# One wide selection in place of sixteen narrow ones in two expert searches, and unread products of a constant table ahead of four norms' transposes

## The chip, the cores and the metric
One core of a Trainium2 chip runs the whole kernel. The metric is the device time of one execution in microseconds. Four compute engines matter here: PE (TensorE, matrix products), DVE (VectorE), ACT (ScalarE) and POOL (GpSimd); SP issues most of the loads. PE's clock has two levels, 1.2 and 2.4 GHz, and the profile gives the granted clock as a share of the upper one (0.50 and 1.00).

## The reference, cut to what matters
256 tokens of width 1024 pass one block (stick-breaking attention, then a mixture of 32 experts) and two further layers. Each of the two layers is a mixer (attention) and a retrieval of single-neuron experts:

```python
q = (ht @ w_q).reshape(T, PEER_HEADS, 2, PEER_QDIM // 2)
s = jnp.einsum('thpd,pnd->thpn', q, sub_keys).astype(jnp.float32)
top_s, top_i = lax.top_k(s, PEER_TOPK)
cand_s = top_s[:, :, 0, :, None] + top_s[:, :, 1, None, :]
cand_i = top_i[:, :, 0, :, None] * PEER_NKEYS + top_i[:, :, 1, None, :]
best_s, best_j = lax.top_k(cand_s.reshape(T, PEER_HEADS, -1), PEER_TOPK)
experts = jnp.take_along_axis(cand_i.reshape(T, PEER_HEADS, -1), best_j, axis=-1)
gates = jax.nn.softmax(best_s, axis=-1)
```

There are 8 heads, 128 keys per half query and 16 results. Then every chosen expert's activation is `gelu(x . u[e])`, and the layer adds the gated sum of `v[e]`. Ahead of each mixer and each retrieval the tokens are normed: x divided by its root mean square, scaled and shifted.

## The kernel before, in words
Tokens lie on 128 partitions in two halves (`th`). Most products are in three passes of a 32-bit format: `mm3` (L211 to L216) takes operands split into a high and a low part. `split` (L167 to L180) makes the high part on ACT (L173) and the low part on DVE (L177) or POOL (L179).

`norm_T` (L384) makes the normed and transposed tokens. It takes the reciprocal root `r`, scales the tokens on DVE into `xs` (L395, or L405 where the sums come with the residual), transposes 16 blocks of 128 x 128 on PE by products with the identity (L412) into four PSUM banks, and from each bank ACT makes `hT` (L417) and DVE its high part `hh` (L418) and low part `hl` (L419). It runs six times: for the first mixer, for the expert mixture (bank tag "o"), for the even mixer (tag "v", with `pre`), for the odd mixer, and ahead of both retrievals ("f0" and "f1", L1437).

`peer` (L1215) is the retrieval. It has a dense form: all 16384 experts are computed in 128 tiles of 128 experts. A tile (`act_tile`, L1239) loads 128 rows of `u`, splits them (`puh` on ACT, `pul` on POOL while the route runs and on DVE later), makes 24 products of 256 columns, and stores `gelu` of the sums. `peer_route` (L1128) runs beside the first 30 tiles and finds the experts and their gates:
- eight projections of two heads' queries, each followed by the scores against the keys (L1145), copied to `s` on ACT (L1147);
- for each half of the tokens and each of 16 half-heads the 16 best scores `tv` and their places `ti` (L1155 to L1159, DVE);
- `tif`, the places as numbers (L1161);
- for each head the 256 sums `cand` (L1165), and their 16 best `bv` and places `bj` (L1172 to L1176);
- the row and column of each place, `ju` and `jf` (L1179, L1181), and for each head and each of the two a selection: compare a running number with `jf` (L1185), multiply by `tif` (L1187), sum (L1188);
- the best score subtracted (L1190), the Exp (L1192, ACT), its sum and quotient (L1194 to L1196), six transposes of `rows` (L1201), and `idx` and `gate` from them.

The order around it is set by three things. Instructions of one engine run in program order as a scheduler laid them. `tiles(N_EXP)` puts 23 tiles ahead of the Exp, which by an explicit dependency stands behind the gelu of the 23rd on ACT (L1192). `tiles(N_TR)` puts seven more ahead of the transposes of `rows`, which stand behind the last product of the seventh (`k.mm`, L1201). After the route, 64 groups of four tokens make one-hot tables `oh` (L1269) and `og`, and PE makes from them the gates of all experts; `iob` (L1226) is the table of running numbers in bf16 for that.

The lines that the steps of the prediction touch are these:

```python
        tiles(N_EXP)
        after(k, nc.scalar.activation(gt, gt, AF.Exp), k.gelu)
...
        tiles(N_TR)
...
                after(k, nc.tensor.transpose(pt[:, c * P:(c + 1) * P], rows[:, th, c, :], k.ident), k.mm)
```

Of the kernel before, what the change touches and what calls it, by code (L numbers as in the profile page):

```python
# [21 lines left out]
P = 128  # L22
# [85 lines left out]
def setup(tc, ctx, aps):  # L108
# [17 lines left out]
    for n, w in SMALL:  # L126
        setattr(k, n, sm[:, off:off + w])
        off += w
    return k
# [254 lines left out]
def norm_T(k, g, sc, sh, tag, pre=None, xs=None, hT=None):  # L384
# [7 lines left out]
    if pre is None:  # L392
        r = x_rstd(k, xs)
        for th in range(2):
            nc.vector.tensor_scalar_mul(xs[:, th, :], k.x[:, th, :], r[:, th:th + 1])  # L395
    else:
# [7 lines left out]
        for th in range(2):  # L404
            nc.vector.tensor_scalar_mul(xs[:, th, :], xg[:, th, :], r[:, 2 + th:3 + th])  # L405
        for th in range(2):
            nc.scalar.activation(k.x[:, th, :], xg[:, th, :], AF.Copy, scale=r[:, th:th + 1])
    for dp in range(4):
        ps = bank(k, tag)
        for j in range(2):  # L410
            for th in range(2):
                nc.tensor.transpose(ps[:, j * T + th * P:j * T + th * P + P],  # L412
                                    xs[:, th, (2 * dp + j) * P:(2 * dp + j + 1) * P], k.ident)
# [714 lines left out]
def peer_route(k, l, idx, gate, tiles):  # L1128
# [3 lines left out]
    with ExitStack() as st:  # L1132
# [15 lines left out]
        rows = one([P, 2, 3, P], "rows")  # L1148
        bvs = one([P, 2, 8, 16], "bv")
        for th in range(2):  # L1150
# [9 lines left out]
            tif = one([P, 8, 2, 16], f"tif{th}")  # L1160
            nc.vector.tensor_copy(tif.rearrange("p h a j -> p (h a) j"), ti)  # L1161
            tvv = tv.rearrange("p (h a) j -> p h a j", a=2)
            cand = tmp(k, pool, [P, 8, 16, 16], "cand", bufs=2)
            for h in range(8):
                nc.vector.tensor_tensor(cand[:, h], tvv[:, h, 0, :, None].to_broadcast([P, 16, 16]),  # L1165
                                        tvv[:, h, 1, None, :].to_broadcast([P, 16, 16]), ALU.add)
            bv = bvs[:, th]
            bj = one([P, 8, 16], f"bj{th}", U32)
            for h in range(8):
# [6 lines left out]
                nc.vector.max_index(bj[:, h, 8:], bv[:, h, 8:], c2)  # L1176
            for p, (op, arg) in enumerate(((ALU.logical_shift_right, 4), (ALU.bitwise_and, 15))):
                ju = one([P, 8, 16], f"ju{th}{p}", U32)
                nc.vector.tensor_scalar(ju, bj, arg, None, op0=op)  # L1179
                jf = one([P, 8, 16], f"jf{th}{p}")  # L1180
                nc.vector.tensor_copy(jf, ju)  # L1181
                o = rows[:, th, p, :].rearrange("p (h j) -> p h j", h=8)
                for h in range(8):
                    eq = tmp(k, pool, [P, 16, 16], "eq", bufs=2)
                    nc.vector.tensor_tensor(eq, k.iota[:, None, :16].to_broadcast([P, 16, 16]),  # L1185
# [318 lines left out]
```

## Time and profile before

| what | value |
|---|---|
| time, median of 3 runs | 2853.11 us (2849.63 to 2861.27) |
| time of the profiled execution | 2850.77 us |
| its span, first to last instruction | 2848.8 us |
| PE busy | 2621.2 us (92%), granted clock 0.961 on average |
| DVE busy | 1901.9 us (67%) |
| ACT busy | 1254.1 us (44%) |
| POOL busy | 391.5 us (14%) |

The span is cut by stages: the first mixer lasts to about 211 us, the expert mixture to 736, the even mixer to 905, the first retrieval to 1790, the odd mixer to 1958, and the second retrieval to the end. In each retrieval the route takes the first 190 us, the gates of all experts the next 300, the weighted sum of `v` the last 390. Busy shares are averages over these stages. What ends a wait in a stage is read from the waits and from the order in time.

### The profile page before, as it was taken

What the parts mean: (1) busy time and instruction counts of PE and PEld (TensorE: products, weight loads), DVE (VectorE), ACT (ScalarE), POOL (GpSimd) and SP (SyncE); (2) the same over time, 40 slices, a digit from 0 to 9 for tenths busy, and PEclk for the clock granted to TensorE, in tenths of its full rate; (3) what the DMA queues carried; (4) which work ended last, traced back from release to release, by engine and by line L of the source; (5) the groups of instructions that cost most, each with busy time, mean ns of one, the idle gap of its engine ahead of it and who ended that gap; (6) DMA issues with size and microseconds to landing.
All of it is one profiled execution on the core that took longest, in us unless ns stands there. A gap on an engine that the chain in (4) does not pass through costs nothing.

```text
span 2848.8 us, 47623 instructions
## 1 busy us (share of the span) xinstructions
PE 2621.2 (92%) x17205; PEld 2143.9 (75%) x17205; DVE 1901.9 (67%) x4151; ACT 1254.1 (44%) x2535; POOL 391.5 (14%) x292
## 2 busy tenths in 40 slices
PE   7998999999798968999999999798968999899998
PEld 5873343434587968999978888688958999888886
DVE  6753111111885998777787887756998777687776
ACT  3531000000555534555545555455535555555554
POOL 2220000000234551000000000224650000000000
PEclk9898999999899989999999999899989999999999
DMA  8678999997662445666797887653445666788775
GB/s 349 224 273 335 421 418 418 419 418 315 233 237 87 130 139 176 199 199 197 221 310 250 297 256 232 260 193 106 144 133 174 202 197 202 241 276 250 243 241 162
DMA packets 208150, 696.54 MB, mean 245 GB/s; under 512 B 23143, under 2 KB 91127, under 8 KB 167588
## 3 DMA queue, kind: packets, MB, share of 16 engines
q1 hardware_dynamic: 161108, 641.51, 64.8%
q10 hardware_dynamic: 46800, 51.93, 5.4%
q8 instruction: 137, 2.24, 0.3%
q14 instruction: 105, 0.86, 0.1%
HBM read 655.55 MB, written 37.78 MB: 243 GB/s over the span
## 4 chain that ended last, share of the span: by engine, by line
PE 52%; DVE 11%; DMA 3%; issue 1%; ACT 1%; ACTq 0%; SPq 0%; DVEq 0%
PE o L215 7%; PE o L216 7%; PE o L214 7%; PE u L214 7%; PE u L215 7%; PE u L216 7%; PE w L1278 3%; DVE eq L1187 2%; DMA pada<-in_ada 2%; DVE eq L1185 2%; PE w L214 2%; PE w L215 2%; PE w L216 2%; DVE adaacc L301 1%; DVE rows L1188 1%
## 5 line engine op out<-in xcount | busy, mean ns | idle before, releaser
L214 PE MATMUL u<-hh,puh 128*128 128x256 f32 x2048 | 589.7, 288 | 53.6 <-ACT puh L173 53.6
L173 ACT CAST puh<-pst 128x512 fp32r<-128x512 f32 x768 | 476.4, 621 | 292.4 <-PE u L215 271.2
L216 PE MATMUL u<-hh,pul 128*128 128x256 f32 x2048 | 578.4, 283 | 2.2 <-POOL pul L179 2.1
L215 PE MATMUL u<-hl,puh 128*128 128x256 f32 x2048 | 578.4, 282 | 0.0
L177 DVE TENSOR_TENSOR pul<-pst,puh 128x512 fp32r<-128x512 f32 x648 | 444.7, 687 | 154.0 <-ACT puh L173 153.3
L214 PEld LDWEIGHTS u<-hh,puh 128*128 128x128 f32 x2048 | 389.5, 190 | 54.0 <-ACT puh L173 54.0
L216 PEld LDWEIGHTS u<-hh,pul 128*128 128x128 f32 x2048 | 388.7, 190 | 3.5 <-POOL pul L179 2.9
L215 PEld LDWEIGHTS u<-hl,puh 128*128 128x128 f32 x2048 | 389.7, 190 | 0.0
L173 ACT CAST pvh<-pst 128x512 fp32r<-128x512 f32 x256 | 159.2, 622 | 197.6 <-ACT puh L173 117.7
L177 DVE TENSOR_TENSOR pvl<-pst,pvh 128x512 fp32r<-128x512 f32 x256 | 176.7, 690 | 67.0 <-ACT pvh L173 67.0
L214 PE MATMUL o<-pvh,pwh 128*128 128x512 f32 x512 | 202.4, 395 | 14.5 <-ACT pwh L173 14.5
L216 PE MATMUL o<-pvh,pwl 128*128 128x512 f32 x512 | 200.3, 392 | 1.5 <-DVE pwl L177 1.5
L215 PE MATMUL o<-pvl,pwh 128*128 128x512 f32 x512 | 200.4, 392 | 0.7 <-DVE pvl L177 0.7
L214 PE MATMUL o<-puh,pwh 128*128 128x512 f32 x512 | 200.0, 391 | 0.0
L215 PE MATMUL o<-pul,pwh 128*128 128x512 f32 x512 | 199.9, 390 | 0.0
L216 PE MATMUL o<-puh,pwl 128*128 128x512 f32 x512 | 199.8, 390 | 0.0
L214 PE MATMUL w<-hh,wsph 128*128 128x256 f32 x648 | 191.0, 295 | 7.7 <-ACT wsph L173 2.9
L215 PE MATMUL w<-hl,wsph 128*128 128x256 f32 x648 | 187.7, 290 | 0.0
L216 PE MATMUL w<-hh,wspl 128*128 128x256 f32 x648 | 187.2, 289 | 0.0
L179 POOL TENSOR_TENSOR pul<-pst,puh 128x512 fp32r<-128x512 f32 x120 | 172.3, 1458 | 91.2 <-ACT puh L173 89.5
L736 DVE TENSOR_TENSOR moesg<-moesg,v 128x512 f32<-128x512 f32 x16 | 11.0, 687 | 234.2 <-PE v L731 234.2
L173 ACT CAST pwh<-u 128x256 fp32r<-128x256 f32 x256 | 95.1, 371 | 125.7 <-PE o L215 101.1
(400 smaller groups left out, 5139.9 us busy)
## 6 DMA issues: line engine op xcount, KB each, us to landing
pst<-in_pu SPq DMA_DIRECT2D x256, 512.0 KB, 4.0
pst<-in_pv SPq DMA_DIRECT2D x256, 512.0 KB, 4.6
moeg<-in_moe_g SPq DMA_DIRECT2D x64, 1024.0 KB, 12.6
moeu<-in_moe_u SPq DMA_DIRECT2D x64, 1024.0 KB, 9.9
moed<-in_moe_d SPq DMA_DIRECT2D x64, 1024.0 KB, 11.6
ada<-in_ada SPq DMA_DIRECT2D x56, 1024.0 KB, 7.0
peer_a<-peerA ACTq DMA_DIRECT2D x256, 128.0 KB, 3.5
peerA<-peer_a SPq DMA_DIRECT2D x256, 128.0 KB, 3.9
```

What stands on the lines that cost most here:

```text
L173: ins = nc.scalar.copy(hi, src)
L177: nc.vector.tensor_tensor(lo, src, hi, ALU.subtract)
L179: nc.gpsimd.tensor_tensor(lo, src, hi, ALU.subtract)
L214: mm(out, lhs[0], rhs[0], start=st, stop=True, skip_group_check=True)
L215: mm(out, lhs[0], rhs[1], start=False, stop=True, skip_group_check=True)
L216: k.mm = mm(out, lhs[1], rhs[0], start=False, stop=True, skip_group_check=True)
L301: nc.vector.scalar_tensor_tensor(acc, wt[:, c, :], cond[:, kc, :1], acc, op0=ALU.mult, op1=ALU.add)
L736: nc.vector.tensor_mul(sg, sg, pgu["u"])
L1185: nc.vector.tensor_tensor(eq, k.iota[:, None, :16].to_broadcast([P, 16, 16]), jf[:, h, :, None].to_broadcast([P, 16, 16]), ALU.is_equal)
L1187: nc.vector.tensor_tensor(eq, eq, tif[:, h, p, None, :].to_broadcast([P, 16, 16]), ALU.mult)
L1188: nc.vector.tensor_reduce(o[:, h, :], eq, AX.X, ALU.add)
L1278: nc.tensor.matmul(pg[:, j], oh[:, j, 1].rearrange("p i d -> p (i d)"), og[c][:, j].rearrange("p i d -> p (i d)"), start=j == 0 and c == 0 ...
```

## The change
The diff has four parts.
- `iob`, the bf16 table of running numbers, is made once in `setup` and not once per retrieval.
- `scale_rows` takes the place of the two scalings in `norm_T`: each half of the tokens is scaled in two pieces of 512 columns, the first half on DVE and the second on ACT.
- `keep_warm` issues n products of `iob` with itself, 512 columns each, into a PSUM bank that nobody reads. They stand behind the last product before them and ahead of the transposes: 12 ahead of the expert mixture, 30 ahead of the odd mixer, 24 ahead of each retrieval.
- In `peer_route` the loops over heads go, for the sums `cand` and for the selection. The comparison and the product run over 2048 elements in bf16 (`ia` holds each running number 16 times, `tif` holds each place twice, side by side). The reduction reads `eq` with its last two dimensions exchanged. The subtraction of the best score is made for each half of the tokens, ahead of the selection.

```diff
+def scale_rows(k, dst, src, r):
+
+    for n in range(2):
+        ns = slice(n * 512, (n + 1) * 512)
+        k.nc.vector.tensor_scalar_mul(dst[:, 0, ns], src[:, 0, ns], r[:, 0:1])
+        k.nc.scalar.activation(dst[:, 1, ns], src[:, 1, ns], AF.Copy, scale=r[:, 1:2])
+
+
+def keep_warm(k, n):
+
+    ps = bank(k)
+    t = k.iob.rearrange("p i d -> p (i d)")
+    last = k.mm
+    for _ in range(n):
+        ins = k.nc.tensor.matmul(ps, t, t[:, None, :].to_broadcast([P, 4, P]), start=True, stop=True, skip_group_check=True)
+        after(k, ins, last)
+        last = ins
+    return last
...
-        for th in range(2):
-            nc.vector.tensor_scalar_mul(xs[:, th, :], k.x[:, th, :], r[:, th:th + 1])
+        scale_rows(k, xs, k.x, r)
...
+    last = keep_warm(k, warm) if warm else None
...
-            tif = one([P, 8, 2, 16], f"tif{th}")
-            nc.vector.tensor_copy(tif.rearrange("p h a j -> p (h a) j"), ti)
+            tif = one([P, 2, 8, 16, 2], f"tif{th}", BF16)
+            for p in range(2):
+                nc.vector.tensor_copy(tif[:, p], ti.rearrange("p (h a) j -> p a h j", a=2)[:, p, :, :, None].to_broadcast([P, 8, 16, 2]))
...
-            for h in range(8):
-                nc.vector.tensor_tensor(cand[:, h], tvv[:, h, 0, :, None].to_broadcast([P, 16, 16]),
-                                        tvv[:, h, 1, None, :].to_broadcast([P, 16, 16]), ALU.add)
+            nc.vector.tensor_tensor(cand, tvv[:, :, 0, :, None].to_broadcast([P, 8, 16, 16]),
+                                    tvv[:, :, 1, None, :].to_broadcast([P, 8, 16, 16]), ALU.add)
...
+            nc.vector.tensor_tensor(gt[:, th], bv, bv[:, :, 0:1].to_broadcast([P, 8, 16]), ALU.subtract)
...
-                for h in range(8):
-                    eq = tmp(k, pool, [P, 16, 16], "eq", bufs=2)
-                    nc.vector.tensor_tensor(eq, k.iota[:, None, :16].to_broadcast([P, 16, 16]),
-                                            jf[:, h, :, None].to_broadcast([P, 16, 16]), ALU.is_equal)
-                    nc.vector.tensor_tensor(eq, eq, tif[:, h, p, None, :].to_broadcast([P, 16, 16]), ALU.mult)
-                    nc.vector.tensor_reduce(o[:, h, :], eq, AX.X, ALU.add)
-        gt = rows[:, :, 2, :].rearrange("p t (h j) -> p t h j", h=8)
-        nc.vector.tensor_tensor(gt, bvs, bvs[:, :, :, 0:1].to_broadcast([P, 2, 8, 16]), ALU.subtract)
+                eq = tmp(k, pool, [P, 8, 16, 16], "eq", BF16, bufs=2)
+                nc.vector.tensor_tensor(eq, ia[:, None].to_broadcast([P, 8, 16, 16]), jf[:, :, None, :].to_broadcast([P, 8, 16, 16]), ALU.is_equal)
+                e2 = eq.rearrange("p h a (j d) -> p (h a) j d", d=2)
+                nc.vector.tensor_tensor(e2, e2, tif[:, p].rearrange("p h a d -> p (h a) d")[:, :, None, :].to_broadcast([P, 128, 8, 2]), ALU.mult)
+                nc.vector.tensor_reduce(rows[:, th, p, :].rearrange("p (h j) -> p h j", h=8), eq.rearrange("p h a j -> p h j a"), AX.X, ALU.add)
```

On DVE, in the first retrieval, between two projections, the order before had the search for one head in it (`cand`, `bv`, `bj`, `c`), mixed with the next best scores `tv` and the splitting of a weight block (`wspl`):

```order
L1165 TENSOR_TENSOR cand_9099<-tv_8999 128x256
L1156 MAX_INDEX ti_9230<-tv_9229,s_8418 128x8
L1172 MAX bv_8998<-cand_9099 128x8
L1155 MAX tv_9229<-s_8418 128x8
L1173 MAX_INDEX bj_9108<-bv_8998,cand_9099 128x8
L1174 MATCH_REPLACE c_9115<-bv_8998,cand_9099 128x256
L177 TENSOR_TENSOR wspl_8634<-wT_8623,wsph_8633 128x512
L1175 MAX bv_8998<-c_9115 128x8
L1156 MAX_INDEX ti_9230<-tv_9229,s_8418 128x8
L1176 MAX_INDEX bj_9108<-bv_8998,c_9115 128x8
```

That search stood there for seven heads. In the changed kernel none of it stands between the projections. All eight heads follow the one wide sum, behind the last best score of the first half:

```order
L1184 MAX tv_9047<-s_9139 128x8
L1188 CAST tif_9145<-ti_9048 128x256
L1185 MAX_INDEX ti_9048<-tv_9047,s_9139 128x8
L1191 TENSOR_TENSOR cand_9148<-tv_9047 128x2048
L1188 CAST tif_9145<-ti_9048 128x256
L1198 MAX bv_9046<-cand_9148 128x8 x2
L1199 MAX_INDEX bj_9150<-bv_9046,cand_9148 128x8
L1200 MATCH_REPLACE c_9151<-bv_9046,cand_9148 128x256
```

Further on, DVE made the selection of the first half in 48 instructions of 256 elements; it is six of 2048 now, with the subtraction of the best score (`rows` from `bv`) ahead of them:

```order
L1203 TENSOR_TENSOR rows_9043<-bv_9046 128x128
L1206 TENSOR_SCALAR ju_9200<-bj_9150 128x128
L1206 TENSOR_SCALAR ju_9208<-bj_9150 128x128
L1208 CAST jf_9202<-ju_9200 128x128
L1208 CAST jf_9210<-ju_9208 128x128
L1211 TENSOR_TENSOR eq_9204<-ia_9044,jf_9202 128x2048
L1211 TENSOR_TENSOR eq_9212<-ia_9044,jf_9210 128x2048
L1213 TENSOR_TENSOR eq_9204<-eq_9204,tif_9145 128x2048
L1213 TENSOR_TENSOR eq_9212<-eq_9212,tif_9145 128x2048
L1214 TENSOR_REDUCE rows_9043<-eq_9204 128x128
L1214 TENSOR_REDUCE rows_9043<-eq_9212 128x128
```

The second half has the same eleven rows. Its other work, the best scores behind their first eight, stands behind the first half's selection as it did before.

On PE, ahead of the first retrieval, the transposes (`s` from `xs`) followed the last product of the mixer's output at once. Now the last of 24 products of the table, each with its own loading of the weights, stands ahead of them, and each bank's transposes come together:

```order
L400 LDWEIGHTS iotab
L400 MATMUL w_8361<-iotab 128x512
L433 MATMUL s_8386<-smalls,xs_8341 128x128 x4
L433 MATMUL s_8399<-smalls,xs_8341 128x128 x4
L433 MATMUL s_8412<-smalls,xs_8341 128x128 x4
L216 MATMUL w_8466<-hh,wsph_8320 128x256
L433 MATMUL s_8425<-smalls,xs_8341 128x128 x4
```

The products wait for one thing beside their order, the bank; the transposes still wait for `xs` from both engines.

## Rows read from the trace of the kernel before

**Rows 1.** The page: the chain that ended last, and one group of DVE.

```profile
PE o L215 7%; PE o L216 7%; PE o L214 7%; PE u L214 7%; PE u L215 7%; PE u L216 7%; PE w L1278 3%; DVE eq L1187 2%; DMA pada<-in_ada 2%; DVE eq L1185 2%; PE w L214 2%; PE w L215 2%; PE w L216 2%; DVE adaacc L301 1%; DVE rows L1188 1%
...
L177 DVE TENSOR_TENSOR pul<-pst,puh 128x512 fp32r<-128x512 f32 x648 | 444.7, 687 | 154.0 <-ACT puh L173 153.3
```

**Rows 2.** Busy times by stretch: stretch, us, PE, PEld, DVE, ACT, POOL, clock, DMA.

```profile
983.00:1033.00 50.00, 50.00 (x425) 50.00 (x424) 50.00 (x65) 26.84 (x53) 49.20 (x36) 1.00 0.80 232
1033.00:1086.00 53.00, 25.42 (x192) 24.80 (x190) 52.93 (x190) 14.84 (x28) 20.39 (x15) 0.71 0.31 96
...
2480.00:2849.00 369.00, 352.82 (x1540) 290.06 (x1540) 285.91 (x541) 197.21 (x392) 4.46 (x3) 0.98 0.75 237
```

**Rows 3.** PE's waits, 1030 to 1100: who, for whom, us, times, longest.

```profile
PE u L214 <- ACT puh L173: 26.8, 1, 26.8
PE w L1201 <- DVE rows L1196: 7.3, 1, 7.3
```

**Rows 4.** ACT in time, both layers: start, us, instruction, idle before it.

```profile
1065.44 0.42 ACT L1192 ACTIVATE rows<-rows 128x256 f32<-128x256 f32 x1 [27.78 <-DVE rows L1190]
...
2118.57 0.42 ACT L1192 ACTIVATE rows<-rows 128x256 f32<-128x256 f32 x1 [27.76 <-DVE rows L1190]
```

**Rows 5.** DVE in time, first layer's route, from the last scores on.

```profile
980.06 0.49 DVE L1155 MAX8 tv<-s 128x8 f32<-128x128 f32 x2 [1.46 <-ACT s L1147]
...
982.68 1.09 DVE L1165 TENSOR_TENSOR cand<-tv 128x256 f32<-128x256 f32 x1
983.70 1.39 DVE L1161 CAST tif<-ti 128x256 f32<-128x256 uint32 x1
...
989.39 2.95 DVE L1185 TENSOR_TENSOR eq<-smalls,jf 128x256 f32<-128x256 f32 x2
...
1036.01 0.07 DVE L1159 MATCH_VALUE_LOAD ti<-tv,s 128x8 f32 x1
...
1050.06 0.73 DVE L1172 MAX8 bv<-cand 128x8 f32<-128x256 f32 x2
...
1065.00 0.41 DVE L1190 TENSOR_TENSOR rows<-bv 128x256 f32<-128x256 f32 x1
...
1092.24 0.40 DVE L1194 TENSOR_REDUCE gz<-rows 128x16 f32<-128x256 f32 x1
```

**Rows 6.** DVE's groups by shape, 983 to 1037: count, busy us, mean ns, idle.

```profile
L1187 DVE TENSOR_TENSOR eq<-eq,tif 128x256 f32<-128x256 f32 x16 | 23.6, 1512 | 0.0
...
L1188 DVE TENSOR_REDUCE rows<-eq 128x16 f32<-128x256 f32 x16 | 5.9, 405 | 0.0
```

**Rows 7.** DVE in time: the scaling ahead of the first retrieval and the odd mixer.

```profile
909.00 3.45 DVE L395 TENSOR_SCALAR xs<-x_res,rrow 128x1024 f32<-128x1024 f32 x2
...
1797.30 1.41 DVE L395 TENSOR_SCALAR xs<-x_res,rrow 128x1024 f32<-128x1024 f32 x2
```

**Rows 8.** Instructions on the one-hot tile: count, duration in ns min/median/max, first, last.

```profile
L1274 DVE TENSOR_TENSOR og<-oh,pgates x384: 410/419/428, 1096.8 to 2460.5; 128x512 bf16<-128x512 bf16 x192
L1269 DVE TENSOR_TENSOR oh<-iotab,idxp x128: 678/684/687, 1095.4 to 2459.1; 128x1024 bf16<-128x1024 bf16 x128
```

**Rows 9.** The transposes: PE in time at three norms, and the tile's own row.

```profile
215.42 3.65 PE L412 MATMUL o<-smalls,xs 128*128 128x128 f32 x16 [4.39 <-DVE xs L395]
...
910.89 0.44 PE L412 MATMUL s<-smalls,xs 128*128 128x128 f32 x1 [8.47 <-issue]
...
1798.19 3.74 PE L412 MATMUL s<-smalls,xs 128*128 128x128 f32 x16 [9.29 <-DVE xs L395]
...
L412 PE MATMUL s<-smalls,xs x64: 272/421/478, 12.2 to 1967.5; 128*128 128x128 f32 x64
```

**Rows 10.** Busy times by short stretch, columns as in rows 2.

```profile
906.00:909.00 3.00, 0.00 (x0) 0.00 (x0) 1.50 (x7) 1.93 (x8) 0.03 (x1) 0.50 0.57 224
...
1094.00:1097.00 3.00, 3.00 (x17) 3.00 (x16) 3.00 (x8) 1.34 (x5) 0.00 (x0) 0.55 0.57 167
...
1968.00:1971.00 3.00, 3.00 (x18) 3.00 (x18) 2.21 (x9) 2.24 (x5) 0.00 (x0) 0.58 0.47 190
```

More of the change, by code (lines that the diff above doesn't have):

```diff
@@ L128, in setup @@
         off += w
+    k.iob = k.const.tile([P, P // 2, 2], BF16, name="iotab")
+    nc.vector.tensor_copy(k.iob, k.iota.rearrange("p (i d) -> p i d", d=2))
     return k
@@ L403, in norm_T @@
         r = rsqrt_of(k, v, [P, 4], "rrow2")
-        for th in range(2):
-            nc.vector.tensor_scalar_mul(xs[:, th, :], xg[:, th, :], r[:, 2 + th:3 + th])
+        scale_rows(k, xs, xg, r[:, 2:])
         for th in range(2):
             nc.scalar.activation(k.x[:, th, :], xg[:, th, :], AF.Copy, scale=r[:, th:th + 1])
+    last = keep_warm(k, warm) if warm else None
     for dp in range(4):
@@ L411, in norm_T @@
             for th in range(2):
-                nc.tensor.transpose(ps[:, j * T + th * P:j * T + th * P + P],
-                                    xs[:, th, (2 * dp + j) * P:(2 * dp + j + 1) * P], k.ident)
+                ins = nc.tensor.transpose(ps[:, j * T + th * P:j * T + th * P + P],
+                                          xs[:, th, (2 * dp + j) * P:(2 * dp + j + 1) * P], k.ident)
+                if last is not None:
+                    after(k, ins, last)
         for j in range(2):
@@ L1148, in peer_route @@
         rows = one([P, 2, 3, P], "rows")
+        ia = one([P, 16, 16], "ia", BF16)
+        nc.vector.tensor_copy(ia, k.iota[:, :16, None].to_broadcast([P, 16, 16]))
+        gt = rows[:, :, 2, :].rearrange("p t (h j) -> p t h j", h=8)
         bvs = one([P, 2, 8, 16], "bv")
@@ L1179, in peer_route @@
                 nc.vector.tensor_scalar(ju, bj, arg, None, op0=op)
-                jf = one([P, 8, 16], f"jf{th}{p}")
+                jf = one([P, 8, 16], f"jf{th}{p}", BF16)
                 nc.vector.tensor_copy(jf, ju)
-                o = rows[:, th, p, :].rearrange("p (h j) -> p h j", h=8)
-                for h in range(8):
-                    eq = tmp(k, pool, [P, 16, 16], "eq", bufs=2)
-                    nc.vector.tensor_tensor(eq, k.iota[:, None, :16].to_broadcast([P, 16, 16]),
-                                            jf[:, h, :, None].to_broadcast([P, 16, 16]), ALU.is_equal)
-                    nc.vector.tensor_tensor(eq, eq, tif[:, h, p, None, :].to_broadcast([P, 16, 16]), ALU.mult)
-                    nc.vector.tensor_reduce(o[:, h, :], eq, AX.X, ALU.add)
-        gt = rows[:, :, 2, :].rearrange("p t (h j) -> p t h j", h=8)
-        nc.vector.tensor_tensor(gt, bvs, bvs[:, :, :, 0:1].to_broadcast([P, 2, 8, 16]), ALU.subtract)
+                eq = tmp(k, pool, [P, 8, 16, 16], "eq", BF16, bufs=2)
[3 more added lines that the diff above has]
+                nc.vector.tensor_reduce(rows[:, th, p, :].rearrange("p (h j) -> p h j", h=8), eq.rearrange("p h a j -> p h j a"), AX.X, ALU.add)
         tiles(N_EXP)
@@ L1224, in peer @@
         gates = tmp(k, pool, [P, T // 4, 3, 4, 2], "pgates", BF16, bufs=1)
-        iob = tmp(k, pool, [P, P // 2, 2], "iotab", BF16, bufs=1)
-        nc.vector.tensor_copy(iob, k.iota.rearrange("p (i d) -> p i d", d=2))
+        iob = k.iob
         k.aw = pool
@@ L1407, in program @@
             with norm("e") as k.nw:
-                gs, xs = norm_T(k, k.ng1, k.mod[0][:, 32:40], k.mod[0][:, 24:32], "o")
+                gs, xs = norm_T(k, k.ng1, k.mod[0][:, 32:40], k.mod[0][:, 24:32], "o", warm=12)
                 route = moe_route(k, mx)
@@ L1423, in program @@
                 with norm("m1", "right") as k.nw:
-                    norm_T(k, k.nm1, mod[:, 8:16], mod[:, 0:8], "s")
+                    norm_T(k, k.nm1, mod[:, 8:16], mod[:, 0:8], "s", warm=30)
             k.bg = [ada_vec(k, l + 1, 2, g1), ada_vec(k, l + 1, 4), ada_vec(k, l + 1, 3)]
@@ L1436, in program @@
             with norm(f"f{l}", "right") as k.nw:
-                norm_T(k, (k.nf0, k.nf1)[l], mod[:, 32:40], mod[:, 24:32], "s")
+                norm_T(k, (k.nf0, k.nf1)[l], mod[:, 32:40], mod[:, 24:32], "s", warm=24)
         peer(k, l)
```

2 lines of the change are left out of this document (1 added, 1 removed).

## The prediction
> **What bounds the kernel now.** I read the chain of work that ended last first. The reader is to see that DVE's selection lines L1185, L1187 and L1188, which belong to the two expert searches (`peer_route`), hold 5% of the span, some 140 us [rows 1]. Then the busy table by stretches, to see what PE does meanwhile: fully busy at a granted clock of 1.00 in 983 to 1033, then busy 25.42 of 53 us at 0.71, with DVE busy throughout. The last row of the group is the weighted-sum stage, where PE runs 1540 products of 512 columns in 352.82 us, 0.229 each at nearly the full level [rows 2]. The waits of PE name two holes in the first layer: 26.8 us for `puh` on ACT, and 7.3 us for `rows` on DVE [rows 3]. ACT itself sat 27.78 us in front of its Exp, waiting for DVE's L1190, and 27.76 us in layer two, so the second layer repeats the first [rows 4]. The Exp stands behind the 23rd tile in ACT's queue, and every `puh` cast of the later tiles stands behind the Exp. So the route is bound by DVE, between the last scores and L1190.
>
> DVE's order in time gives that stretch: it waits for the last scores until 980.06 (1.46 us idle) and reaches L1190 at 1065.00, 84.9 us later [rows 5]. In it the selection of the first half of the rows takes from 989.39 to 1036.01, 46.6 us for 48 instructions of 256 elements. The multiplication among them means 1512 ns while POOL works, while a reduction of the same size takes 405 [rows 6]. Since two comparisons stand 2.95 us long and POOL was busy 49.20 of 50 us in that stretch [rows 2, 5], I read this as a wait of about 1.1 us for one POOL instruction in front of each. The wait does not grow with the size: two 1024-element scalings took 3.45 us beside POOL and 1.41 without, 1.0 more each [rows 7].
>
> **The change, part by part: the route.** Per layer, from the last scores to L1190.
> - Removed: 46.6 us. Put in its place: two comparisons and two products of 2048 bf16 elements and two reductions. A bf16 comparison of 1024 takes 0.684 and a product of 512 takes 0.419 [rows 8], 0.265 per 512 more, so 2048 take about 1.2; with the 1.1 wait 2.3, four of them 9.2. A reduction of 2048: 0.405 for 256 [rows 6] and, by the 0.687 of 512-element DVE work [rows 1], 0.28 for each 256 more, 2.4; two are 4.8. New total 14.0, so -32.6.
> - Moved: the search for one head (L1172 to L1176) stood between the projections for seven of eight heads, under a fully busy PE. It now waits for the one large addition, behind the last scores. Eight heads take 1050.06 to 1065.00, 14.9 us [rows 5], so seven add +13.1. What they leave in the projections is worth nothing, since PE is the bound there.
> - The additions `cand`: the first half had one small one in this stretch, 1.09 [rows 5]; now 2.4 + 1.1, +2.4. In the second half eight of at most 0.4 become one of 3.5: +0.6.
> - `tif` is written twice per half. One cast beside POOL takes 1.39 [rows 5]: +1.4 in the first half, +2.4 in the second (POOL then still works, where before it had stopped). L1190 is split in two: +1.4 for the first.
> Sum: -32.6 + 13.1 + 2.4 + 0.6 + 1.4 + 2.4 + 1.4 = **-11.3**. PE's first hole shrinks from 26.8 to about 15.5 us; DVE stays the bound, and PE still starts again at the low level.
>
> The second hole closes. Before, PE finished its seven tiles 7.3 us before DVE's last selection (row 1092.24, plus 1.2 for the reciprocal and product) [rows 3, 5], so at 1086.1, 20.7 us after the Exp. Now DVE needs from L1190 about 4 x 2.3 + 4.8 + 0.7 + 1.2 = 15.9 us at most, under 20.7: cover of 5 us, and what is late next is PE itself. That is **-7.3**, and **-1.4** for the 2.7 of 3 us that PE worked at the low level after that hole (mean 0.55) [rows 10].
>
> What it costs: a DVE instruction of 2048 elements keeps POOL off for 1.2 us rather than 0.3, and POOL feeds `pul` at PE's pace. In the first half PE would lose time, but time in front of a hole, which costs nothing. In the last seven tiles I put **+0.5**; the ends are 0 (PE is at the low level and takes `pul` half as fast) and 4.8 (4 x 1.2). Route: -11.3 - 7.3 - 1.4 + 0.5 = -19.5 per layer, **-39** for two.
>
> Here the Trainium skill speaks against the change: its page "SBUF — State Buffer", section "Who interferes with whom", says that a DVE instruction with two SBUF inputs and a GpSimd one that reads SBUF exclude each other for the whole instruction, whichever starts first. The trace agrees as to DVE's wait (1512 against about 400 ns); by that rule alone the seven tiles would lose the 4.8 end and the route would give 30.4 us.
>
> **The norms.** The 12, 30, 24 and 24 products of 512 columns are hidden in holes where PE waits for `xs`: 4.39, 9.29 and 8.47 us for the first three [rows 9], the fourth like the third. At 0.229 each [rows 2] they take 2.7, 6.9 and 5.5, so they cost nothing. Without that cover, at the low level (twice as long), they would run 1.1 + 4.4 + 2.5 + 2.5 = 10.5 us into the transposes. Before, the transposes ran at the low level (0.50 in 906 to 909): 16 in 3.65 us, median 421 ns, while some at the full level took 272 [rows 9, 10]. With the clock kept, 16 transposes save 1.7 us. `scale_rows` splits 3.45 us of DVE work [rows 7] between DVE and ACT, about 1 us off. After the norm ahead of the first route I count -2.4. Ahead of the second the clock stayed low into the projections (0.58 in 1968 to 1971 [rows 10]), so -4.0. Ahead of the expert mixture ACT's eight `hT` set the pace: -1.2. Ahead of the odd mixer DVE's half-finished vectors and a load follow: -0.5. In the norm without products ACT gets two more instructions in front of `hT`: +0.4. Sum **-7.7**. The table `iotab`, now built once, stood beside POOL's work: 0. The ends are +10.5 (low level) and -12 (all four at 3 us).
>
> The rows show the low level during transposes, but not whether the clock, once kept, would last through the rest of the hole; if it falls there, the norms give about 3 us from the split scaling alone.
>
> Total: 2850.8 - 39 - 7.7 = **2804 us** against the profiled execution; the median of the three runs is 2.3 us above it, well inside their own spread.
>
> **Rivals.**
> - DVE is fast enough. If the 1.1 us waits are mostly absent, L1190 comes before PE's 23rd tile ends, 15.5 us earlier than I put it; then both holes and both low stretches go (0.71 over 53 us is 30.7 us at the low level, 3.9 more than the hole, so at least 2.0 lost): 26.8 + 7.3 + 1.4 + 2.0 = 37.5 per layer, 2850.8 - 75 - 7.7 = 2768. For it: five long instructions meet fewer POOL instructions than 33 short ones. Against: POOL is busy 49.20 of 50 us in the first half.
> - POOL starves PE, the 4.8 end, and the products run at the low level, so that the norms lose 5 instead: 2850.8 - 30.4 + 5 = 2825. For it: POOL has no slack at PE's pace. Against: PE still has a 15 us hole to lose.
> - The products do nothing for the clock: norms -3, 2809.
> - Slower: the reduction now reads `eq` with a step of 16 elements, and no row shows DVE doing that. If one takes X us, L1190 moves from 1053.7 by 2(X - 2.4), and with the 11.1 us of the tail outside its reductions the route ends at 1060 + 4X, against 1093.4 before. Less 3.9 a layer from the norms, it loses from X = 9.3 on; at X = 13 the kernel takes 2850.8 + 37.2 - 7.7 = 2880. For it: nothing but the missing row. Against: the reduction of today shows no cost beyond one element per cycle.
> - The route is not what ended last, so nothing comes of it but the norms, 2843: against it stands PE's idle time [rows 3], which nothing else fills.
>
> **How the numbers follow.** Forecast with its own errors (waits of 0.5 to 1.2 us, norms 3 to 10) 2790 to 2818: 0.63. DVE fast enough 0.12, POOL starves 0.11, nothing for the clock 0.06 (inside the forecast's range), no gain 0.05, slower 0.03. The range 2774 to 2829 leaves out the last three hundredths, the no-gain case and the far end of the fast one. Half a per cent, 14 us, is about what a measurement of this kernel can tell from no change: faster 0.91, same 0.06, slower 0.03.
>
> **What would show it.** ACT's idle time in front of the Exp near 15 us instead of 27.8; PE's wait for `rows` gone; the two reductions near 2.4 us; comparisons of 2048 near 2.3 beside POOL and 1.2 without; the transposes of four norms near 270 ns; PE's clock at 1.00 from the last output product into the projections. A hole of under 5 us in front of the Exp, reductions over 5 us, or long waits of PE for `pul` would show me wrong.

## The result: 2811 us against 2852, and the profile after

| | before | changed |
|---|---|---|
| median | 2851.89 us (4 runs) | 2811.12 us (2797.66 to 2816.29, 4 runs) |
| ratio, 95% interval | | 0.9844 [0.9802, 0.9886] |
| profiled execution, span | 2850.77, 2848.8 us | 2808.32, 2806.5 us |

Forecast were 2804 us and a range of 2774 to 2829. Line numbers move: L1190 before is L1203 now, L1192 is L1216, L1185, L1187 and L1188 are L1211, L1213 and L1214, L412 is L433, L177 and L179 are L179 and L181.

The page of the changed kernel, the chain that ended last. The three lines of the selection, 5% of the chain before [rows 1], are no longer in it. That alone does not clear DVE: the chain passes the hole that is left in front of the Exp as time in which PE waited for nothing visible ("issue", 14.86 us from 1047.92 on), while ACT's row below names DVE's L1203:

```profile
PE u L216 8%; PE u L218 8%; PE u L217 8%; PE o L218 8%; PE o L216 8%; PE o L217 8%; PE w L1301 3%; PE w L216 2%; PE w L217 2%; PE w L218 2%; POOL pul L181 1%; DMA pada<-in_ada 1%; DVE adaacc L303 1%; PE w L1168 1%; PE o L1076 0%
```

PE's waits in the changed kernel, 880 to 1120, to be held against [rows 3] (who, for whom, us in total, times, longest):

```profile
PE u L216 <- ACT puh L175: 12.1, 1, 12.1
PE u L218 <- POOL pul L181: 5.0, 7, 0.9
```

The hole in front of the Exp is less than half as long, the one for `rows` is gone, and small waits for `pul` have come in. ACT in time shows the same in both layers, 14.15 us of idle time for 27.78 and 27.76 [rows 4]:

```profile
1061.69 0.42 ACT L1216 ACTIVATE rows<-rows 128x256 f32<-128x256 f32 x1 [14.15 <-DVE rows L1203]
...
2084.45 0.42 ACT L1216 ACTIVATE rows<-rows 128x256 f32<-128x256 f32 x1 [14.15 <-DVE rows L1203]
```

DVE in time, first layer, from the last scores to the end of its tail (to be held against [rows 5]):

```profile
986.74 0.49 DVE L1181 MAX8 tv<-s 128x8 f32<-128x128 f32 x2 [4.07 <-ACT s L1170]
...
990.20 3.11 DVE L1191 TENSOR_TENSOR cand<-tv 128x2048 f32<-128x2048 f32 x1
...
1010.76 1.45 DVE L1206 TENSOR_SCALAR ju<-bj 128x128 uint32<-128x128 uint32 x2
1012.13 1.48 DVE L1208 CAST jf<-ju 128x128 bf16<-128x128 uint32 x2
1013.53 3.44 DVE L1211 TENSOR_TENSOR eq<-ia,jf 128x2048 bf16<-128x2048 bf16 x2
1016.90 4.52 DVE L1213 TENSOR_TENSOR eq<-eq,tif 128x2048 bf16<-128x2048 bf16 x2
1021.35 8.50 DVE L1214 TENSOR_REDUCE rows<-eq 128x128 f32<-128x2048 bf16 x2
1029.70 0.14 DVE L1185 MATCH_VALUE_LOAD ti<-tv,s 128x8 f32 x1
...
1061.38 0.27 DVE L1203 TENSOR_TENSOR rows<-bv 128x128 f32<-128x128 f32 x1
...
1077.93 1.52 DVE L1220 TENSOR_TENSOR rows<-rows,gz 128x256 f32<-128x256 f32 x1
```

From the last scores to the second L1203 it is 74.64 us, 84.94 before: -10.3. The first comparison came 17.5 us later after the last scores (26.79 for 9.33), the selection from there took 16.17 for 46.62, and the second half 31.68 for 28.99. Rows and columns (`ju`, `jf`) stand ahead of the first comparison in both kernels; before, they were

```profile
987.76 0.34 DVE L1179 TENSOR_SCALAR ju<-bj 128x128 uint32<-128x128 uint32 x2
988.02 1.46 DVE L1181 CAST jf<-ju 128x128 f32<-128x128 uint32 x2
```

The tile `eq` by itself (duration in ns min/median/max, first and last start):

```profile
L1211 DVE TENSOR_TENSOR eq<-ia,jf x8: 1212/1750/2309, 1013.5 to 2086.0; 128x2048 bf16<-128x2048 bf16 x8
L1213 DVE TENSOR_TENSOR eq<-eq,tif x8: 1211/2298/2300, 1016.9 to 2090.4; 128x2048 bf16<-128x2048 bf16 x8
L1214 DVE TENSOR_REDUCE rows<-eq x8: 4196/4290/4477, 1021.3 to 2095.7; 128x128 f32<-128x2048 bf16 x8
```

By stages (from PE's first product after one norm's transposes to its last before the next norm, the last stage to the end of the span; a hole is PE's time from its last product ahead of a norm to the first one behind the norm's transposes, unread products not counted, summed over the five norms behind the first):

| us | before | changed | once more | route alone | norms alone | no products |
|---|---|---|---|---|---|---|
| up to the first stage | 29.7 | 28.3 | 30.3 | 28.8 | 27.5 | 29.9 |
| first mixer | 181.4 | 181.6 | 182.0 | 181.9 | 181.7 | 180.4 |
| expert mixture | 499.6 | 499.1 | 499.1 | 499.4 | 499.1 | 496.4 |
| even mixer | 162.7 | 173.2 | 172.0 | 174.2 | 173.1 | 173.3 |
| first retrieval | 873.6 | 853.0 | 857.1 | 855.0 | 875.5 | 858.6 |
| odd mixer | 153.8 | 146.5 | 146.7 | 153.9 | 145.4 | 146.5 |
| second retrieval | 881.2 | 861.7 | 863.5 | 862.1 | 880.2 | 862.0 |
| five holes | 66.9 | 63.0 | 62.9 | 66.7 | 62.2 | 63.2 |
| span | 2848.8 | 2806.5 | 2813.7 | 2822.1 | 2844.8 | 2810.3 |

The last four columns are the first four experiments below. Between before and the change the retrievals give -40.1, the holes -3.9, the odd mixer -7.3; the even mixer takes 10.5 back. In some executions the clock is low for some 25 us in the even mixer's attention, and the times of one kernel form two groups some 10 to 14 us apart (beside the repeat of the change, nine of 17 of the kernel before lie at 2848.6 to 2852.1 and eight at 2862.3 to 2866.6, three of six of the changed kernel at 2798.2 to 2800.9 and three at 2811.9 to 2815.5), so that group against group the change is worth 51 us.

### The profile page after: what moved, and what is told of

It is laid out like the page before. It is cut to its first block, busy times and chain, and to the rows that moved or that the text cites. A ratio compares the mean times of both kernels' runs of the same rounds, so it can differ in the third digit from the quotient of the medians.

```text
span 2806.5 us, 47623 instructions
## 1 busy us (share of the span) xinstructions
PE 2638.0 (94%) x17295; PEld 2144.6 (76%) x17295; DVE 1812.4 (65%) x3962; ACT 1261.0 (45%) x2547; POOL 394.0 (14%) x292
## 4 chain that ended last, share of the span: by engine, by line
PE 60%; DVE 2%; issue 2%; DMA 2%; POOL 1%; ACT 1%; SPq 0%; ACTq 0%; POOLq 0%; DVEq 0%
PE u L216 8%; PE u L218 8%; PE u L217 8%; PE o L218 8%; PE o L216 8%; PE o L217 8%; PE w L1301 3%; PE w L216 2%; PE w L217 2%; PE w L218 2%; POOL pul L181 1%; DMA pada<-in_ada 1%; DVE adaacc L303 1%; PE w L1168 1%; PE o L1076 0%
## 5 line engine op out<-in xcount | busy, mean ns | idle before, releaser
L216 PE MATMUL u<-hh,puh 128*128 128x256 f32 x2048 | 588.3, 287 | 24.2 <-ACT puh L175 24.2
L179 DVE TENSOR_TENSOR pul<-pst,puh 128x512 fp32r<-128x512 f32 x648 | 444.6, 687 | 156.7 <-ACT puh L175 156.1
L179 DVE TENSOR_TENSOR pvl<-pst,pvh 128x512 fp32r<-128x512 f32 x256 | 176.6, 690 | 66.2 <-ACT pvh L175 65.9
L181 POOL TENSOR_TENSOR pul<-pst,puh 128x512 fp32r<-128x512 f32 x120 | 172.0, 1448 | 60.8 <-ACT puh L175 54.0
```

Source lines behind the costliest of these rows:

```text
L179: nc.vector.tensor_tensor(lo, src, hi, ALU.subtract)
L181: nc.gpsimd.tensor_tensor(lo, src, hi, ALU.subtract)
L216: mm(out, lhs[0], rhs[0], start=st, stop=True, skip_group_check=True)
```

## The experiments

All times are medians; the ratio is to the kernel before, which was measured anew beside each set of runs: 2852.07 us for the parts of the change, 2861.38 for five more tiles, the reduction, the search and the longer products, 2858.62 for the kernel before with more tiles and the joined kernels. Across these sets the ratios and the stages of the traces are to be compared, not the medians.

### The parts of the change, one at a time

**Once more**, no edit.

> The changed kernel once more, unaltered. In its first profile the clock stood at 0.50 through 860 to 884 us, in the even mixer's attention with PE busy, where the kernel before shows 1.00; that mixer took 173.2 us from its first to its last product against 162.7. Theory A: that stretch comes by chance in some executions, so here the mixer takes about 163 us again, and times from 2797 to 2816 us occur. Theory B: the change causes it (its products, or where the work stands in time), so the stretch is there again, at about the same place, and the mixer takes 172 to 174.

Measured: 2806.38 us (2798.20 to 2815.51), 0.9819 [0.9788, 0.985]. In the trace the even mixer took 172.0 us, as theory B has it; the times reach from 2798 to 2816 us, as theory A has it. The next run decides.

**Route alone**:

```diff
-        scale_rows(k, xs, k.x, r)
+        for th in range(2):
+            nc.vector.tensor_scalar_mul(xs[:, th, :], k.x[:, th, :], r[:, th:th + 1])
...
-                gs, xs = norm_T(k, k.ng1, k.mod[0][:, 32:40], k.mod[0][:, 24:32], "o", warm=12)
+                gs, xs = norm_T(k, k.ng1, k.mod[0][:, 32:40], k.mod[0][:, 24:32], "o")
```

and so at the other scaling and the three other norms.

> The route's part alone: no unread products, and the scaling of the norms as in the kernel before. Theory (the forecast): the route is worth 39 us by itself, the first trace of the change has the two retrievals 40.1 us shorter, so 2852 - 40 = 2812, and within 4 us the same as the whole change, since its norms brought only 3.8 in the holes. Rival 1: the route needs the products, because it begins with projections that otherwise run at the low level; then 2820 or more. Rival 2: the products cost more than they bring (the even mixer's low stretch is theirs), then 2800 to 2805, faster than the whole change.

Measured: 2809.79 us, 0.984 [0.9807, 0.9873]. The retrievals are 37.7 us shorter than before, the odd mixer is as before (153.9). The trace is of one of two long executions (2824.08 and 2825.90; the other four took 2805.07 to 2810.94), so the median, which agrees with that of the whole change, stands for other executions than the trace, whose span is 8.4 and 15.6 us longer than the change's two.

This run decides on the even mixer. But for the table `iob` made in `setup`, its program is that of the kernel before up to the route, and in the even mixer all four engines run the same instructions in the same order; yet the clock fell. Busy times by stretch of route alone (stretch, us, PE, PEld, DVE, ACT, POOL, clock, DMA):

```profile
860.00:888.00 28.00, 26.44 (x84) 16.38 (x84) 14.03 (x48) 11.67 (x41) 4.33 (x8) 0.51 0.00 1
```

and from the same place of the mixer on in the last experiment of the next section, whose mixer has again the instructions of before:

```profile
860.00:885.00 25.00, 22.91 (x139) 16.64 (x139) 16.20 (x54) 14.75 (x47) 6.62 (x11) 1.00 0.05 22
```

Of the 14 traces of this study five show the even mixer at 162 to 163 us (the kernel before among them) and nine at 172 to 174, with the clock at 0.51 to 0.57 over these 28 us. So the 10.5 us are not the change's. The kernel before itself has one trace only, without that stretch; that it has the stretch in other executions is read from its two groups of times. What tips the clock there stays open.

**Norms alone**: the changed kernel with `peer_route` of the kernel before.

> The other parts alone: the unread products and the divided scaling, with the route of the kernel before. Theory (the forecast): -7.7, so about 2844. By the holes of the first trace of the change (six norms, -3.8 in all): about 2848. Rival: nothing, or slower, if the low stretch in the even mixer comes with the products: 2855 to 2860.

Measured: 2846.94 us (12 runs), 0.9961 [0.994, 0.9982]: a small gain, with the even mixer's low stretch in its trace. The holes fell by 4.7 us, the odd mixer by 8.4.

**No products**: `warm=12`, `warm=30` and `warm=24` taken out, nothing else.

> The whole change without the unread products; the divided scaling and the route stay. Theory (the forecast): the products keep the clock and are worth about 4 us of the 7.7, so 2815 against the whole change's 2811, with the transposes of all norms at about 421 ns. Rival: the clock falls between the products and the transposes in most norms (in the first trace it did in two of four), so they are worth 0 to 2 us: 2811 to 2813. In both, the scaling in halves alone takes 1 us off each hole.

Measured: 2810.66 us, 0.9839 [0.9811, 0.9866], between the two medians of the whole change (2811.12 and 2806.38). Its five holes are 63.2 us, against 63.0 and 62.9 with the products. What the norms gave came from the scaling in halves. The odd mixer goes with it too: 145.4 to 146.7 us in the four traces of the table that have it, 153.8 and 153.9 in the two that don't. With it the scheduler laid the odd mixer's instructions out anew; PE's 1062 rows of that stretch differ from those of route alone from the 218th on. That this order is what saves the 7 us was not tested by itself.

The table shows a cost of the products as well: without them the expert mixture takes 496.4 us, with them 499.1 (499.4 in route alone, which has neither them nor the scaling in halves). The hole ahead of it is 5.95 us with them and 7.28 without, but then PE waits 2.0 us for `hh` where without them it doesn't. So ahead of the mixture they cost more than they bring.

### The terms of the route

**Five more tiles** ahead of the Exp:

```diff
-N_EXP, N_TR = 23, 7
+N_EXP, N_TR = 28, 7
```

> The changed kernel with 28 tiles ahead of the Exp in place of 23. Theory: what is left of the route's price is PE's hole of 12.1 us a layer in front of the Exp, which is DVE's time to L1203 and nothing else. A tile takes PE 2.84 us, five take 14.2, so the hole closes; DVE's L1203 comes no later, ACT's idle time before the Exp falls from 14.2 to about 0, and the two layers give 2 x 12.1 and some 2 us of low clock behind each hole: 2808 - 28 = 2780. Rival: the tiles are then missing later, in the stage of the gates, where DVE (225 of 300 us busy) or the loads become the bound, and the time comes back: 2800 or more.

Measured: 2790.66 us, 0.9747 [0.9722, 0.9773]. PE's wait for `puh` is gone in both layers. The retrievals are 18.6 us shorter than the change's, not 28. PE's waits from 1066 to 1770, and in the route, 915 to 1110:

```profile
PE o L216 <- ACT pwh L175: 10.2, 1, 10.2
...
PE u L218 <- POOL pul L181: 5.4, 9, 0.8
```

The first stands between the gates and the weighted sum; with 23 tiles its longest is 7.1. So 24.2 us of hole go, and some 3 us a layer come back where the tiles are missing, which gives the 18: the rival has a small part in it.

**The reduction in order**:

```diff
-            tif = one([P, 2, 8, 16, 2], f"tif{th}", BF16)
...
+            tif = one([P, 8, 2, 16], f"tif{th}", BF16)
+            nc.vector.tensor_copy(tif.rearrange("p h a j -> p (h a) j"), ti)
...
+                jf = one([P, 8, 16, 2], f"jf{th}{p}", BF16)
+                nc.vector.tensor_copy(jf, ju[:, :, :, None].to_broadcast([P, 8, 16, 2]))
...
+                nc.vector.tensor_tensor(eq.rearrange("p h j (a d) -> p (h j) a d", d=2), k.iob[:, None, :8, :].to_broadcast([P, 128, 8, 2]),
+                                        jf.rearrange("p h j d -> p (h j) d")[:, :, None, :].to_broadcast([P, 128, 8, 2]), ALU.is_equal)
+                nc.vector.tensor_tensor(eq, eq, tif[:, :, p, None, :].to_broadcast([P, 8, 16, 16]), ALU.mult)
-                nc.vector.tensor_reduce(rows[:, th, p, :].rearrange("p (h j) -> p h j", h=8), eq.rearrange("p h a j -> p h j a"), AX.X, ALU.add)
+                nc.vector.tensor_reduce(rows[:, th, p, :].rearrange("p (h j) -> p h j", h=8), eq, AX.X, ALU.add)
```

> The changed kernel with `eq` laid out so that the reduction reads neighbouring elements; the two numbers of a pair now come from `jf`, written twice, and not from `tif`. The forecast took 2.4 us for a reduction of 2048; the first trace of the change shows 4.2 to 4.5, with POOL and without. Theory: the step of 16 elements (32 bytes) costs the difference, so a reduction now takes about 2.1 us, the first half's two make L1203 come 4.3 us earlier, and both holes of 12.1 us shrink by as much: 2808 - 9 = 2799. Rival: the price is that of a reduction from bf16 as such; it stays at 4.2 and the time does not change.

Measured: 2802.26 us, 0.9795 [0.9768, 0.9822]. The reduction on the tile `eq`, and ACT in front of the Exp:

```profile
L1211 DVE TENSOR_REDUCE rows<-eq x8: 2268/2272/2273, 1019.9 to 2086.0; 128x128 f32<-128x2048 bf16 x8
```

```profile
1055.97 0.42 ACT L1213 ACTIVATE rows<-rows 128x256 f32<-128x256 f32 x1 [7.39 <-DVE rows L1200]
```

The same 2048 numbers take 2.27 us in order and 4.29 with the step of 32 bytes, so the rival is out. From the first projection to L1200 it is 134.0 us for 139.5: 4.0 of the 5.5 come from the first half's two reductions, most of the rest from `tif`, which is cast once in each half and no longer twice (1.2 and 0.7 us less). ACT's idle time fell by 6.8 us and not by 5.5, since ACT also came to it 1.3 us later. PE's hole is 6.4 us in both layers, and the retrievals are 7.8 us shorter than the change's. The Trainium skill's page "SBUF — State Buffer", section "Door 1: The DMA port swizzle", says that a line of SBUF holds 16 bytes and that each access in a new line pays a penalty, 8 bf16 being the reach without. The two rows agree, and give the size for this reduction: 2.0 us; no run here has a step within such a line.

**The search by head**:

```diff
-            nc.vector.tensor_tensor(cand, tvv[:, :, 0, :, None].to_broadcast([P, 8, 16, 16]),
-                                    tvv[:, :, 1, None, :].to_broadcast([P, 8, 16, 16]), ALU.add)
+            for h in range(8):
+                nc.vector.tensor_tensor(cand[:, h], tvv[:, h, 0, :, None].to_broadcast([P, 16, 16]),
+                                        tvv[:, h, 1, None, :].to_broadcast([P, 16, 16]), ALU.add)
```

> The changed kernel with the sums `cand` made head by head again, as before the change; the selection stays wide. The forecast put +13.1 us a layer on the search of seven heads that the wide sum moved behind the last scores, under the limit of PE's hole. Theory: with the search back between the projections L1203 comes 13 to 15 us earlier, the hole of 12.1 us closes and so does most of the low clock behind it: 2808 - 26 = 2782. Rival: the search delays the splitting of the projections' weights on DVE, PE waits for `wspl`, and the projections grow by up to 8 x 1.9 = 15 us a layer, so nothing is gained: 2800 to 2815.

Measured: 2793.88 us, 0.9767 [0.9743, 0.979]; the retrievals are 16.5 us shorter than the change's. No wait for `wspl` appears in the projections. ACT's idle time is half as long, but not gone. The selection of the first half starts 15.3 us earlier after the last scores, as the theory had it. But in the second half the eight small sums stand beside POOL and take 10.3 us in place of 2.91, the last six of them in one row of DVE in time:

```profile
1020.43 7.60 DVE L1192 TENSOR_TENSOR cand<-tv 128x256 f32<-128x256 f32 x6
```

```profile
1043.20 0.42 ACT L1217 ACTIVATE rows<-rows 128x256 f32<-128x256 f32 x1 [7.07 <-DVE rows L1204]
```

Small sums in the first half and a wide one in the second would have both; that wasn't tried.

**The kernel before with more tiles**, nothing else:

```diff
-N_EXP, N_TR = 23, 7
+N_EXP, N_TR = 33, 10
```

> The kernel before with nothing changed but 33 and 10 tiles in place of 23 and 7. Theory: PE's loss in the route is the two holes of 26.8 and 7.3 us and the low clock around them, whatever DVE does in that time; ten tiles of 2.84 us fill the first and three more the second. So PE never stops, and the old selection costs nothing: 2856 - 2 x 37 = 2782, less what PE then waits at the end of the gates (3 us a layer or more, since fewer tiles are left for that stage): 2788, faster than the change. Rival 1: DVE's selection becomes longer beside a POOL that works on for thirteen more tiles, the holes stay in part: 2810. Rival 2: the stage of the gates, with 85 tiles in place of 98, is bound by DVE, and gives 2800 or more.

Measured: 2809.93 us, 0.9835 [0.9813, 0.9857], the time of the change and not less than it. Its retrievals are 55.7 us shorter than before, against 40.1 with the change and 34.2 in its repeat; the holes at the norms and the odd mixer stay as before. ACT in time, first layer, and PE's waits from 920 to 1760:

```profile
1073.89 0.42 ACT L1192 ACTIVATE rows<-rows 128x256 f32<-128x256 f32 x1 [7.18 <-DVE rows L1190]
```

```profile
PE u L214 <- ACT puh L173: 6.2, 1, 6.2
PE o L214 <- ACT pwh L173: 5.1, 1, 5.1
PE w L1201 <- DVE rows L1196: 4.7, 1, 4.7
```

Both holes stay in part, as the first rival had it, but not through the selection. L1190 came 157.1 us after the first projection, 149.7 before, since POOL now works on beside the second half's small sums. Their group on DVE, 1037 to 1073 (busy, mean ns, idle):

```profile
L1165 DVE TENSOR_TENSOR cand<-tv 128x256 f32<-128x256 f32 x8 | 9.6, 1249 | 0.0
```

Before, with POOL at rest, the eight took 2.9 us (403 ns each), while the selection's 16 products mean 1513 ns here and 1512 there. The theory's 2 x 37 us less what the two holes keep (6.2 and 4.7 us, in the second layer 6.5 and 3.3) is 53, near the 55.7. So what the route's part gained is PE's idle time and no more, and two numbers fill more of it than the rewritten search did.

### Products up to the transposes

```diff
-                gs, xs = norm_T(k, k.ng1, k.mod[0][:, 32:40], k.mod[0][:, 24:32], "o", warm=12)
+                gs, xs = norm_T(k, k.ng1, k.mod[0][:, 32:40], k.mod[0][:, 24:32], "o", warm=17)
...
-                    norm_T(k, k.nm1, mod[:, 8:16], mod[:, 0:8], "s", warm=30)
+                    norm_T(k, k.nm1, mod[:, 8:16], mod[:, 0:8], "s", warm=46)
...
-                norm_T(k, (k.nf0, k.nf1)[l], mod[:, 32:40], mod[:, 24:32], "s", warm=24)
+                norm_T(k, (k.nf0, k.nf1)[l], mod[:, 32:40], mod[:, 24:32], "s", warm=(36, 33)[l])
```

> The changed kernel with more unread products, 17, 46, 36 and 33 in place of 12, 30, 24 and 24, so that at 0.229 us each they end when `xs` comes. In the first two traces of the change they ended 2.9 us before the transposes ahead of the first retrieval and 3.7 ahead of the odd mixer, and there the transposes still took about 421 ns; 1.2 us ahead of the mixture, and there they took 273. Theory: the gap decides; without it the transposes take 273 in all four norms and each of the two norms gives 2 us more: 2804. Rival 1: the late products push the transposes back by what they gain, no change. Rival 2: the clock in the mixers moves the time by more than this, +-10, and nothing can be told from the medians; then the holes in the trace tell it.

Measured: 2813.32 us, 0.984 [0.9816, 0.9865]: no gain. PE in time at the transposes, in the changed kernel at the mixture, the first retrieval, the odd mixer and the second retrieval:

```profile
213.97 2.04 PE L433 MATMUL o<-smalls,xs 128*128 128x128 f32 x16 [1.19 <-DVE xs L390]
...
918.75 2.79 PE L433 MATMUL s<-smalls,xs 128*128 128x128 f32 x12 [2.88 <-issue]
...
1785.18 3.54 PE L433 MATMUL s<-smalls,xs 128*128 128x128 f32 x16 [3.77 <-DVE xs L390]
...
1942.47 1.50 PE L433 MATMUL s<-smalls,xs 128*128 128x128 f32 x12 [2.27 <-DVE xs L390]
```

and with the longer products, at the first retrieval and the odd mixer:

```profile
909.89 1.50 PE L433 MATMUL s<-smalls,xs 128*128 128x128 f32 x12 [0.30 <-issue]
...
1776.23 1.47 PE L433 MATMUL s<-smalls,xs 128*128 128x128 f32 x12
```

Twelve transposes take 1.50 us at the full level and 2.79 where most ran at the low one, so the products do keep the clock if they last. Yet a hole is only 0.8 us shorter ahead of the first retrieval than in the changed kernel and 1.5 ahead of the odd mixer (12.01, against 11.81 with no products at all), none ahead of the second retrieval. The first product behind them waits for `hh`, not for a transpose. In that trace the odd mixer took 156.6 us, with stretches at 0.74 and 0.70; rival 2 holds.

### The terms joined

```diff
-N_EXP, N_TR = 23, 7
+N_EXP, N_TR = 24, 5
```

with the edits of the reduction in order and of the search by head.

> The changed kernel with the reduction in order, the search head by head, and 24 and 5 tiles in place of 23 and 7. Theory: the hole that the search by head left is 6.1 us a layer, the reductions in order take 4.2 of it and one more tile of 2.84 the rest, so PE never stops in front of the Exp; the tail behind the Exp is 4.3 us shorter and five tiles (14.2 us) cover it. Against the search by head alone (2794) that is 2 x 6 and the low clock behind the hole: 2780. Rival: PE then waits longer at the end of the gates, as with five more tiles (10.2 us for `pwh` against 7.1), or for `pul` from POOL, and the sum stays at 2788.

Measured: 2773.63 us (2765.56 to 2780.35), 0.9695 [0.9671, 0.972], below both kernels. No idle time stands in front of the Exp:

```profile
1050.39 0.42 ACT L1214 ACTIVATE rows<-rows 128x256 f32<-128x256 f32 x1
```

What is left of PE's waits in the first retrieval:

```profile
PE o L216 <- ACT pwh L175: 5.8, 1, 5.8
PE u L218 <- POOL pul L181: 3.5, 7, 0.5
```

So the longer wait for `pwh` that the rival expected did not come.

**The joined kernel without the unread products**: `warm` taken out at the four norms.

> As the joined kernel (reduction in order, search by head, 24 and 5 tiles), without the unread products. Theory, by the holes of the norms in the traces so far: the products bring 1.3 us ahead of the mixture, 0.7 ahead of the second retrieval, nothing ahead of the first, and cost 1 ahead of the odd mixer, so together 1 us at most: the same time as with them, +-3. Rival: they are worth the 4 us by which the change with them read lower once than without: then 4 us slower.

Measured: 2781.50 us, 0.973 [0.9708, 0.9751]. The medians lie 7.9 us apart, but they stand for different executions. Here all five (2777.67 to 2784.66) lie by the traced one, which has the low stretch in the even mixer; with products two do (2778.64 and the traced 2780.35, with that stretch), three took 2765.56 to 2773.63. The two traces read 2780.35 with products and 2777.67 without, the mixture being 499.1 and 496.3 us. So the 7.9 us do not show a worth of the products. Whether it is chance that no execution without them was short is not settled.

**The joined kernel with longer products**: `warm=17` ahead of the mixture, `warm=(36, 33)[l]` ahead of the retrievals, none ahead of the odd mixer.

> As the joined kernel, with 17, 36 and 33 products that end when `xs` comes, and none ahead of the odd mixer. Theory: by the holes of the norms this is the best set, 0.8 us ahead of the first retrieval, 0.7 ahead of the second and 1 to 2 ahead of the odd mixer under the joined kernel with the change's products: 2 to 3 us faster. Rival: the medians do not show it, since the clock in the mixers moves the time by 10 us from one execution to the next.

Measured: 2774.14 us, 0.9704 [0.968, 0.9728]: as the joined kernel. Its five holes are 61.0 us for 63.1.

## Why the prediction was right, point by point

- **DVE bounds the route, and PE's holes are the price**: shown by closing or narrowing them in four ways (five more tiles, reduction in order, search by head, more tiles in the kernel before). Each moved the retrievals by roughly what it took off the holes: 18.6 us for 24.2, 7.8 for 11.4, 16.5 for 12.0, 55.7 for 47.5.
- **-11.3 us to L1190**: measured -10.3. The term that was mis-sized is the reduction, put at 2.4 us and measured at 4.2 to 4.5, from the step that the forecast met only in its rival; in order it took 2.27. The selection took 16.2 us for the 14.0 forecast and so gave 30.4 and not 32.6: the two reductions were 8.5 for 4.8, and part of that came back because the two comparisons were 3.4 for 4.6 (one took 2.3, as put, the other 1.2, as without a wait for POOL). The work ahead of the selection grew by 17.5 us for the 18.3 of its four terms (search, `cand`, casts, L1190), and the second half by 2.7 for 3.0.
- **The first hole to 15.5 us**: 12.1 for PE, 14.15 for ACT. PE came to it 4.3 us later, 3.3 of that in waits for `pul`. That is the POOL term, placed where the forecast said it costs nothing. Behind the Exp PE waited 1.7 us for `pul` (0.8 before), between the 0.5 taken and the end of 4.8 that the prediction put beside the rule of the Trainium skill's page "SBUF — State Buffer", section "Who interferes with whom".
- **The second hole closes**: it did. DVE's tail took 18.1 us from L1203 on for 15.9, the reductions again; 17.3 of it lie behind the Exp, under PE's 20.7.
- **-39 for the route**: from the first projection behind the norm to the first one-hot table it was 180.1 and 181.0 us and is 163.0 and 162.9, so -35.2; the retrievals as wholes are 34 to 40 us shorter in four traces, the difference lying mostly in the first layer's weighted sum behind (358.4 us in the changed kernel's first trace, 363.0 in its repeat, 359.8 before).
- **-7.7 for the norms**: wrong in its parts. The holes gave 3.9, and as much without the products (3.7): the step "with the clock kept, 16 transposes save 1.7 us" failed twice, because in two of four norms the clock fell in the gap between the last product and `xs`, and because a shorter run of transposes is hardly a shorter hole. "They cost nothing" failed ahead of the mixture, which is 2.7 us longer with them. The rival in which the products do nothing for the clock was right in this (-3), with what the scaling alone gives; its 2809 us and the forecast's 2804 can't be told apart by the change's two medians.
- **Not foreseen**: -7.3 in the odd mixer, which comes with the scaling and an order of instructions that the scheduler changed far from the edit; +10.5 in the even mixer, by the clock and not by the change. That -46.7 stands so near the -42.3 of the profiled executions is in part luck: these two lie beside it. Like against like the change is worth 51 us; the route came close to its 39 in mechanism and size, and the odd mixer's 7.3 more than made up for the 3.8 that the norms' 7.7 lacked.

## What to carry to other kernels

Where an engine stands idle for another, first see whether independent work can be put into the hole by a number; here two numbers took 55.7 us off the retrievals, the rewritten search 40.1, and the joined kernel, which has both kinds of edit, 69.5. When narrow instructions become a wide one, look at what leaves the shade of other work (the search of seven heads), at the step in which the reduction reads, and at how often an instruction has to wait for another engine rather than at how much it computes. A repeated profile of a program that is the same up to some point tells which differences are not the edit's.

## What the runs showed of the hardware

- A reduction of 2048 bf16 on DVE takes 2.27 us with neighbouring elements and 4.2 to 4.5 with a step of 32 bytes, with POOL at work and without.
- A sum of 256 elements on DVE takes 403 ns with POOL at rest and 1249 beside it; one of 2048 takes 2.7 to 3.3, so beside POOL eight small ones cost some 7 us more than a large one.
- PE's clock fell to 0.50 for 24 to 27 us with PE nearly always busy (26.44 of 28 us in route alone), in the even mixer's attention, in nine of 14 traces and at the same place of the program; in the other five it stayed at 1.00.
- The gap ahead of the transposes does not alone decide on the clock: seven traces have 24 products and then 2.27 us of idle time ahead of the second retrieval's transposes, and these ran at the full level in four (272 ns each in the changed kernel) and wholly or partly at the low one in three (median 421 in its repeat); behind 3.8 us ahead of the odd mixer they took 421 in the changed kernel and most took 273 in norms alone.
